# One of three Strassen weight tiles made in DRAM by adding copies instead of on DVE, in a fp32 transformer-layer kernel

## The chip, the cores and the metric

The kernel runs on one core of a Trainium2 chip. The metric is the time of one execution on the device in microseconds, median of three runs. Beside the timed runs there is one profiled execution, from which every row below comes. Engines are named as the profile names them: PE does matmuls (PEld loads their stationary operand), DVE elementwise vector work, ACT activations and copies, POOL a little elementwise work and one DMA queue (q0), SP nothing but the other DMA queue (q1).

## The reference

One layer of a transformer-like trunk on x of 256 x 2048 in fp32: a normalised input projection, two mixers (a gated linear recurrence and chunked attention), gates, an output projection, and a SwiGLU feed-forward block. Cut to the products that matter here:

```
h = rms_norm(x, norm_mix)
proj = h @ w_in                               # 2048 x 11264, the last 4096 columns are gate logits
gate_a, gate_b = split(sigmoid(proj[gates] + b_gate))
merged = gate_a * (y_a @ w_proj_a) + gate_b * (y_b @ w_proj_b)
x = x + merged @ w_out                        # 2048 x 2048
h = rms_norm(x, norm_ffn)
ff_gate, ff_up = split(h @ w_ffn_in)          # 2048 x 11264
x = x + (silu(ff_gate) * ff_up) @ w_ffn_out   # 5632 x 2048
```

## The kernel before, in words

All large products stream their weights from DRAM in tiles of 128 partitions x 2 x 512 floats (512 KB, `raw`, 8 buffers), fetched by SP (`fetch`, L130). A fp32 product is made of three reduced-precision matmuls: each operand is split into a high half `hi` (a copy by ACT, L177) and a low half `lo` (a subtraction by DVE, L178), and `triple` issues hi x hi, hi x lo, lo x hi (L222 to L224). The activation side is the stationary operand, so a matmul streams 512 columns of weights. `hi` and `lo` of the weights have 4 buffers each.

A block of work is a chunk: four k-tiles of a 512-column block of weights. `product` does 24 matmuls for each chunk and each 512 columns. `product_pair` takes two column blocks at once and, on some chunks, replaces the eight triples of k-tiles 0 and 1 by seven, by a scheme of Strassen's kind. This use of the scheme needs sums of four weight blocks. In the names of `weight_forms`: b11 and b21 are k-tiles 0 and 1 of the first column block, b12 and b22 those of the second. Three of the seven weight operands are b11, b21 and b22 themselves, two are in a tile `ta` (b12-b11 and b22-b12) and two in a tile `tb` built from `ta`. DVE makes all four sums (L194, one instruction for each half of a tile), and each tile is then split into `hi` and `lo` like a fetched one. `ta` and `tb` share a pool `t6` of two buffers. On the activation side `act_forms` makes four sums for each use, kept for the whole stretch; the feed-forward ones are stored to DRAM (L315) and loaded again (L907) by POOL's queue.

There are 46 uses: 8 in two gate pairs (4 chunks each), 4 in the first out pair, 20 in the five `w_fi` pairs j = 1, 3, 5, 7, 9 (4 chunks each; the even j are plain products of the same length between them), and 14 in the two `w_fo` pairs (7 of 11 chunks each). In the profiled execution the PE work of these pairs starts at 407 and 492 us (gates), 623 (out), 757, 843, 930, 1017 and 1104 (`w_fi`), 1190 and 1312 (`w_fo`). In all but the `w_fo` pairs the first chunk's plain half is done before its seven triples (`plain_first`).

The order of instructions on each engine is fixed when the program is built: a scheduler places them by priority and by a time model; weight preparation has a raised priority (`PREP_AHEAD`). A buffer is fetched anew when the last reader of its old content is done, and SP issues its DMAs strictly in their order, waiting at each for its buffer.

Of the kernel before, what the change touches and what calls it, by code (L numbers as in the profile page):

```python
# [45 lines left out]
def block_kernel(ctx: ExitStack, tc: tile.TileContext, x, x_t, w_in, w_pa, w_pb, w_out, w_fi, w_fo,  # L46
# [53 lines left out]

    def rsqrt_mean(dst, ss, n):
# [22 lines left out]
    def fetch(w, nb, kc, n=2, pinned=False):  # L124

        res = []
        for hf in range(2):
            raw = wraw_p.tile([P, 2, 512], F32, tag="raw", name=nm("raw"))
# [6 lines left out]
        return res  # L135

# [51 lines left out]
    def weight_forms(r0, r1):  # L188


        ta = t6_p.tile([P, 2, 512], F32, tag="t6", name=nm("ta"))
        tb = t6_p.tile([P, 2, 512], F32, tag="t6", name=nm("tb"))
        b11, b21, b12, b22 = r0[:, 0, :], r0[:, 1, :], r1[:, 0, :], r1[:, 1, :]
        op = lambda out, x, y, o: nc.vector.tensor_tensor(out=out, in0=x, in1=y, op=o)  # L194
        p1, p2 = halves(r0)
        p3, = halves(r1[:, 1:2, :])
# [8 lines left out]
    def product_pair(w, nbs, n_chunks, act, forms, c_pool, u_pool, epilogue, plain_first=False,  # L205
                     last=False):

        tag = {id(mm): "mm", id(aux): "bank"}  # L210
# [36 lines left out]
        for kc in range(n_chunks):  # L247
            end = kc == n_chunks - 1
            early = plain_first and kc == 0
            with tc.high_priority(offset=min(PREP_AHEAD, tc.cur_priority - first_block[0])):  # L250
                r = [fetch(w, nb, kc) for nb in nbs]
                ws = [[None] * 4 for _ in nbs]
                if kc not in forms:
                    for n in range(2):
                        ws[n][0:2] = halves(r[n][0])
                        ws[n][2:4] = halves(r[n][1])
                else:
                    if not early:
                        tf = weight_forms(r[0][0], r[1][0])
                    for n in range(2):  # L260
                        ws[n][2:4] = halves(r[n][1])
                    if early:
                        tf = weight_forms(r[0][0], r[1][0])
# [43 lines left out]
    def transpose_split(nat, hi, lo, gain=None, wait=2, pool=aux, forms=None, spill=None):  # L307
        for _ in range(wait):
            yield 1
        for pair in range(2):  # L310
            pt = transpose_split_pair(nat, pair, hi, lo, gain, pool)
            if forms is not None and pair == 0:
                act_forms(pt, forms, gain)
                if spill is not None:
                    nc.gpsimd.dma_start(out=spill, in_=forms.bitcast(F32))  # L315
            yield 1

    def act_forms(pt, f, gain=None):

# [10 lines left out]
        if gain is None:  # L330
            nc.scalar.copy(s[:, 2, :], a21)
        else:
            nc.scalar.activation(s[:, 2, :], a21, AF.Copy, scale=gain[:, 0:1])
        op(s[:, 0, :], a22, 1, s[:, 2, :], ALU.add)
        op(s[:, 2, :], a11, 0, s[:, 2, :], ALU.subtract)
# [654 lines left out]
```

## Time and profile before

| | |
|---|---|
| median of three runs | 1428.98 us (1428.71 to 1429.38) |
| the profiled execution, time and span | 1427.22 us, 1425.4 us |
| PE / PEld / DVE / ACT / POOL busy | 1417.6 / 1174.4 / 1063.6 / 774.2 / 50.1 us |
| SP's queue q1, POOL's queue q0 | 274.66 MB, 12.58 MB |
| share of the 16 DMA engines, q1 / q0 | 57.5% / 2.3% |

The span is the time from the first to the last instruction of the profiled execution; that execution's own time is 1.8 us more, and lies 1.8 us below the median. Busy time is summed over a whole execution; where an engine that is not the busiest one makes PE wait shows only in windows, waits and timelines.

### The profile page before, as it was taken

How to read it: one execution, taken by the hardware profiler on the slowest of the kernel's cores; microseconds unless marked ns; L12 is line 12 of the kernel's file. 1: busy time of each engine (PE TensorE's matmuls, PEld its weight loads, DVE VectorE, ACT ScalarE, POOL GpSimd, SP SyncE). 2: the span in 40 equal slices, each digit the busy share in tenths (PEclk: the TensorE clock that was granted, in tenths of full speed). 3: DMA queues.
4: the chain of work that ended last, by engine and by line, in shares of the span. 5: the costliest groups of instructions: out<-in, count | busy, mean ns of one | idle time of the engine just before them, and what ended most of it. 6: DMA issues, size and time to landing. Idle time of an engine off the chain costs nothing.

```text
span 1425.4 us, 17596 instructions
## 1 busy us (share of the span) xinstructions
PE 1417.6 (99%) x6448; PEld 1174.4 (82%) x6448; DVE 1063.6 (75%) x1361; ACT 774.2 (54%) x1009; POOL 50.1 (4%) x63
## 2 busy tenths in 40 slices
PE   9999999999999999999999999999999999999998
PEld 7888888888888888878888888888788888888887
DVE  6768869564878697689767769687796876777875
ACT  7756565555655454455555546455454554544553
POOL 0100100100000000100000000000000010000000
PEclk9999999999999999999999999999999999999999
DMA  9654354446657556547654657656476578666652
GB/s 360 243 192 161 134 193 156 164 163 195 222 183 240 197 197 210 184 148 239 220 203 168 228 169 240 206 179 228 164 238 206 178 254 303 210 221 221 208 183 84
DMA packets 81848, 288.37 MB, mean 202 GB/s; under 512 B 9185, under 2 KB 9441, under 8 KB 81761
## 3 DMA queue, kind: packets, MB, share of 16 engines
q1 hardware_dynamic: 78272, 274.66, 57.5%
q0 software_dynamic: 3488, 12.58, 2.3%
q8 instruction: 50, 0.82, 0.2%
q14 instruction: 38, 0.30, 0.1%
HBM read 279.34 MB, written 7.86 MB: 201 GB/s over the span
## 4 chain that ended last, share of the span: by engine, by line
PE 98%; DVE 1%; ACT 0%; DMA 0%; issue 0%; SPq 0%; DVEq 0%; ACTq 0%
PE mm L169 18%; PE mm L168 18%; PE mm L170 18%; PE mp L223 13%; PE mp L224 13%; PE mp L222 13%; PE bank L285 2%; PE bank L543 1%; DVE wlo L178 1%; ACT whi L177 0%; PE bank L573 0%; DMA raw<-in_w_in 0%; PE bank L619 0%; PE bank L670 0%; PE bank L698 0%; DVE tb L194 0%
## 5 line engine op out<-in xcount | busy, mean ns | idle before, releaser
L148 DVE TENSOR_TENSOR wlo<-raw,whi 128x1024 fp32r<-128x1024 f32 (+1 forms) x292 | 351.9, 1212 | 175.6 <-ACT whi L147 173.4
L147 ACT CAST whi<-raw 128x1024 fp32r<-128x1024 f32 (+1 forms) x292 | 301.9, 1040 | 292.7 <-PE mm L170 219.8
L178 DVE TENSOR_TENSOR wlo<-raw,whi 128x1024 fp32r<-128x1024 f32 x216 | 235.0, 1110 | 51.9 <-ACT whi L177 50.8
L177 ACT CAST whi<-raw 128x1024 fp32r<-128x1024 f32 x216 | 201.2, 960 | 121.8 <-PE mp L224 59.6
L168 PE MATMUL mm<-whi,xTh 128*128 128x512 f32 x576 | 226.6, 398 | 1.3 <-ACT whi L147 1.3
L169 PE MATMUL mm<-wlo,xTh 128*128 128x512 f32 x576 | 225.2, 391 | 0.0
L170 PE MATMUL mm<-whi,xTl 128*128 128x512 f32 x576 | 225.1, 391 | 0.0
L168 PE MATMUL mm<-whi,x2Th 128*128 128x512 f32 x384 | 150.0, 391 | 0.0
L170 PE MATMUL mm<-whi,x2Tl 128*128 128x512 f32 x384 | 149.5, 389 | 0.0
L169 PE MATMUL mm<-wlo,x2Th 128*128 128x512 f32 x384 | 149.4, 389 | 0.0
L168 PEld LDWEIGHTS mm<-whi,xTh 128*128 128x128 f32 x576 | 108.2, 188 | 23.0 <-ACT whi L147 2.0
L170 PEld LDWEIGHTS mm<-whi,xTl 128*128 128x128 f32 x576 | 108.2, 188 | 22.6
L169 PEld LDWEIGHTS mm<-wlo,xTh 128*128 128x128 f32 x576 | 108.3, 188 | 21.8 <-DVE wlo L148 1.0
L223 PE MATMUL mp<-wlo,hTh 128*128 128x512 f32 x282 | 109.7, 389 | 0.0
L224 PE MATMUL mp<-whi,hTl 128*128 128x512 f32 x282 | 109.6, 389 | 0.0
L222 PE MATMUL mp<-whi,hTh 128*128 128x512 f32 x282 | 99.7, 390 | 0.0
L177 ACT CAST whi<-ta 128x1024 fp32r<-128x1024 f32 x46 | 48.3, 1050 | 89.9 <-PE mp L224 87.4
L178 DVE TENSOR_TENSOR wlo<-ta,whi 128x1024 fp32r<-128x1024 f32 x46 | 56.2, 1223 | 48.3 <-ACT whi L177 48.3
L224 PE MATMUL mp<-whi,x2Tl 128*128 128x512 f32 x220 | 86.2, 392 | 0.0
L223 PE MATMUL mp<-wlo,x2Th 128*128 128x512 f32 x220 | 86.2, 392 | 0.0
L170 PEld LDWEIGHTS mm<-whi,x2Tl 128*128 128x128 f32 x384 | 72.1, 188 | 15.0
L168 PEld LDWEIGHTS mm<-whi,x2Th 128*128 128x128 f32 x384 | 72.1, 188 | 14.8
(256 smaller groups left out, 2260.8 us busy)
## 6 DMA issues: line engine op xcount, KB each, us to landing
raw<-in_w_fi SPq DMA_DIRECT2D x176, 512.0 KB, 4.4
raw<-in_w_in SPq DMA_DIRECT2D x172, 512.0 KB, 4.1
raw<-in_w_fo SPq DMA_DIRECT2D x88, 512.0 KB, 5.3
raw<-in_w_out SPq DMA_DIRECT2D x32, 512.0 KB, 4.3
raw<-in_w_pa SPq DMA_DIRECT2D x16, 512.0 KB, 3.7
raw<-in_w_pb SPq DMA_DIRECT2D x16, 512.0 KB, 4.3
x<-x POOLq DMA_DIRECT2D x8, 512.0 KB, 5.7
kept<-sform POOLq DMA_DIRECT2D x7, 512.0 KB, 4.9
```

Source lines behind the costliest of these rows:

```text
L147: nc.scalar.copy(hi[:, sl, :], src[:, sl, :])
L148: nc.vector.tensor_tensor(out=lo[:, sl, :], in0=src[:, sl, :], in1=hi[:, sl, :].bitcast(F32), op=ALU.subtract)
L168: nc.tensor.matmul(ps[m], lhsT=ah, rhs=wh, start=kc == 0 and k4 == 0, stop=False)
L169: nc.tensor.matmul(ps[m], lhsT=ah, rhs=wl, start=False, stop=False)
L170: nc.tensor.matmul(ps[m], lhsT=al, rhs=wh, start=False, stop=kc == n_chunks - 1 and k4 == 3)
L177: nc.scalar.copy(hi, src)
L178: nc.vector.tensor_tensor(out=lo, in0=src, in1=hi.bitcast(F32), op=ALU.subtract)
L222: nc.tensor.matmul(ps, lhsT=ah, rhs=wh, start=first, stop=False)
L223: nc.tensor.matmul(ps, lhsT=ah, rhs=wl, start=False, stop=False)
L224: nc.tensor.matmul(ps, lhsT=al, rhs=wh, start=False, stop=final)
L285: nc.tensor.transpose(out=pt[:, j, m * P:(m + 1) * P], in_=nat[:, m, c:c + P], identity=ident)
L543: nc.tensor.matmul(pl[:, j, :], lhsT=ek[:, g // 2, (g % 2) * P:(g % 2 + 1) * P], rhs=eq[:, g, :], start=True, stop=True)
```

## The change

The tile `ta` is no longer made by DVE. `make_sums`, on POOL's queue, makes it in DRAM: for each use two copies of 256 KB from the weights to a DRAM tile (L160), then one DMA of 512 KB that adds the two k-tiles of the second block onto it (L162). To make this possible every sum is a plain addition. It is called at the start of a pair for a later pair, behind a small copy on POOL that waits for a result of the pair that ended (`begin_mark`): at the start of gate pair 1 for out, of gate pair 3 for `w_fi` j = 1, of out for j = 3, of j = 1, 3, 5 for j = 5, 7, 9, and of j = 7 and 9 for the two `w_fo` pairs, 7 uses each; the gates' own sums are made before them. `fetch_pair` then takes five `raw` buffers for a use where there were four: k-tiles 0 and 1 of the first block, b22 alone (256 KB), the finished sum from DRAM, and the two plain halves.

```diff
+    def make_sums(n, mark):
+        pinned = tc.keep_in_program_order
+        if to_make:
+            pinned(nc.gpsimd.tensor_copy(begin_mark, mark))
+        for _ in range(min(n, len(to_make))):
+            name, w, nbs, chunks = to_make.pop(0)
+            for kc in chunks:
+                t = sums_t[name, nbs[0], kc] = dram.tile(
+                    [P, 2, 512], F32, tag=f"sum_{name}{nbs[0]}_{kc}", name=nm("sum"))
+                for n in range(2):
+                    pinned(nc.gpsimd.dma_start(out=t[:, n, :], in_=w[nbs[n], kc, :, 0, :]))
+            for kc in chunks:
+                pinned(nc.gpsimd.dma_start(out=sums_t[name, nbs[0], kc],
+                                           in_=w[nbs[1], kc, :, 0:2, :], accum_op=ALU.add))
+    def fetch_pair(name, w, nbs, kc):
+        b1, b22, ta = raw_tile(), raw_tile(), raw_tile()
+        nc.sync.dma_start(out=b1, in_=w[nbs[0], kc, :, 0:2, :])
+        nc.sync.dma_start(out=b22[:, 1, :], in_=w[nbs[1], kc, :, 1, :])
+        nc.sync.dma_start(out=ta, in_=sums_t[name, nbs[0], kc])
+        rest = []
+        for nb in nbs:
+            rest.append(raw_tile())
+            nc.sync.dma_start(out=rest[-1], in_=w[nb, kc, :, 2:4, :])
+        return (ta, b1, b22), rest
...
-        op(ta[:, 0, :], b12, b11, ALU.subtract)
-        op(ta[:, 1, :], b22, b12, ALU.subtract)
         p5, p7 = halves(ta)
-        op(tb[:, 0, :], ta[:, 0, :], b22, ALU.subtract)
-        op(tb[:, 1, :], b21, tb[:, 0, :], ALU.add)
+        add(tb[:, 0, :], ta[:, 0, :], b22[:, 1, :])
+        add(tb[:, 1, :], b1[:, 1, :], tb[:, 0, :])
...
+        make_sums(1, mark)
...
-                    nc.gpsimd.dma_start(out=spill, in_=forms.bitcast(F32))
+                    nc.sync.dma_start(out=spill, in_=forms.bitcast(F32))
...
-        op(s[:, 0, :], a22, 1, s[:, 2, :], ALU.add)
+        op(s[:, 0, :], a22, 1, s[:, 3, :], ALU.subtract)
...
-        add(e01, ub[6], e00)
-        add(e10, ub[7], e01)
+        sub(e01, ub[6], e00)
+        sub(e10, e01, ub[7])
...
-            nc.gpsimd.dma_start(out=xs[nb], in_=x2_kept[nb])
+            nc.sync.dma_start(out=xs[nb], in_=x2_kept[nb])
```

The other lines of the diff swap additions and subtractions one for one where results are put together, and move the loads of x for the gates' forms, the stores of x2, and the reloads of the stored forms from POOL's queue to SP's, as the two pairs of lines above do.

In the program's order the change shows at pair j = 5 on DVE. Before, between the splits of chunk 0's `ta` and chunk 1's `tb` (`hTl` is the low half of the transposed previous block):

```order
L178 TENSOR_TENSOR wlo_7755<-ta_7742,whi_7754 128x1024 [waits Activation_49]
L194 TENSOR_TENSOR ta_7839<-raw_7835,raw_7831 128x512 [waits DMAHW7_49,DMAHW1_49,DVE_49]
L194 TENSOR_TENSOR ta_7839<-raw_7835 128x512
L295 TENSOR_TENSOR hTl_7724<-bank_7778,hTh_7723 128x512 [waits Activation_49]
L178 TENSOR_TENSOR wlo_7761<-tb_7743,whi_7760 128x1024 [waits Activation_49]
L295 TENSOR_TENSOR hTl_7724<-bank_7799,hTh_7723 128x512 [waits Activation_49]
L194 TENSOR_TENSOR tb_7840<-ta_7839,raw_7835 128x512 [waits DVE_49]
L178 TENSOR_TENSOR wlo_7842<-raw_7831,whi_7841 128x1024 [waits Activation_49]
L178 TENSOR_TENSOR wlo_7846<-raw_7835,whi_7845 128x512 [waits Activation_49]
L194 TENSOR_TENSOR tb_7840<-raw_7831,tb_7840 128x512 [waits DVE_49]
L178 TENSOR_TENSOR wlo_7852<-ta_7839,whi_7851 128x1024 [waits Activation_49]
L178 TENSOR_TENSOR wlo_7858<-tb_7840,whi_7857 128x1024 [waits Activation_49]
```

and after, from the split of chunk 0's sum (raw_7845) to that of chunk 1's `tb` (tb_7957); raw_8029, raw_8030 and raw_8031 are b1, b22 and the sum of chunk 2:

```order
L218 TENSOR_TENSOR wlo_7871<-raw_7845,whi_7870 128x1024 [waits Activation_49]
L332 TENSOR_TENSOR hTl_7824<-bank_7894,hTh_7823 128x512 [waits Activation_49]
L218 TENSOR_TENSOR wlo_7877<-tb_7861,whi_7876 128x1024 [waits Activation_49]
L332 TENSOR_TENSOR hTl_7824<-bank_7915,hTh_7823 128x512 [waits Activation_49]
L99 TENSOR_TENSOR tb_8039<-raw_8031,raw_8030 128x512 [waits DMAHW6_49,DMAHW5_49,DVE_49]
L218 TENSOR_TENSOR wlo_7959<-raw_7947,whi_7958 128x1024 [waits Activation_49]
L218 TENSOR_TENSOR wlo_7963<-raw_7948,whi_7962 128x512 [waits Activation_49]
L99 TENSOR_TENSOR tb_8039<-raw_8029,tb_8039 128x512 [waits DMAHW4_49,DVE_49]
L218 TENSOR_TENSOR wlo_7967<-raw_7949,whi_7966 128x1024 [waits Activation_49]
L218 TENSOR_TENSOR wlo_7973<-tb_7957,whi_7972 128x1024 [waits Activation_49]
```

The two `ta` subtractions of chunk 1 are gone, and the place of chunk 1's first `tb` operation is taken by chunk 2's, which now waits for DMAs; chunk 1's four splits stand behind it as before.

PE's order there is the same in both but for the numbers; these are the matmuls that take the low halves of chunk 1's `ta` (wlo_7852) and `tb` (wlo_7858), as before has them:

```order
L223 MATMUL mp_7816<-wlo_7852,fx_5593 128x512 [waits DVE_49]
L224 MATMUL mp_7816<-whi_7851,fx_5593 128x512
L223 MATMUL mp_7820<-wlo_7852,fx_5593 128x512
L224 MATMUL mp_7820<-whi_7851,fx_5593 128x512
L222 MATMUL mp_7764<-whi_7861,x2Th_5591 128x512 [waits Activation_49]
L223 MATMUL mp_7824<-wlo_7858,fx_5593 128x512 [waits DVE_49]
```

Nothing moves there; the DVE instructions that they wait for now stand behind the waiting addition.

On POOL's queue a `w_fi` pair now begins with this, after, at the start of j = 1 (sums 6398 to 6407 are those of the four chunks of j = 5); before, POOL had one store of forms (L315) in such a pair or none:

```order
L153 COPY begin_mark<-hn_6243 128x1 [waits DVE_49]
L160 DMA sum_6398<-in_w_fi 128x512 x2
L160 DMA sum_6401<-in_w_fi 128x512 x2
L160 DMA sum_6404<-in_w_fi 128x512 [waits DMASW0_49]
L160 DMA sum_6404<-in_w_fi 128x512 [waits DMASW1_49]
L160 DMA sum_6407<-in_w_fi 128x512 [waits DMASW2_49]
L160 DMA sum_6407<-in_w_fi 128x512 [waits DMASW3_49]
L162 DMA sum_6398<-in_w_fi 128x1024 [waits DMASW5_49,DMASW4_49]
L162 DMA sum_6401<-in_w_fi 128x1024 [waits DMASW7_49,DMASW6_49]
L162 DMA sum_6404<-in_w_fi 128x1024 [waits DMASW1_49,DMASW0_49]
L162 DMA sum_6407<-in_w_fi 128x1024 [waits DMASW3_49,DMASW2_49]
```

Each adding DMA waits on POOL until its own two copies have landed. The sum of chunk 2 is fetched by SP (raw_8031) into the buffer of raw_7845, which is free once the first instruction of the DVE piece of after above, the split into wlo_7871, has read it.

## Rows read from the trace of the kernel before

**Rows 1.** The page of the whole execution: span, engines' busy time, granted clock, DMA queues.

```profile
span 1425.4 us, 17596 instructions
...
PE 1417.6 (99%) x6448; PEld 1174.4 (82%) x6448; DVE 1063.6 (75%) x1361; ACT 774.2 (54%) x1009; POOL 50.1 (4%) x63
...
PEclk9999999999999999999999999999999999999999
...
q1 hardware_dynamic: 78272, 274.66, 57.5%
```

**Rows 2.** Windows: us, busy us (instructions) of PE, PEld, DVE, ACT, POOL; clock, DMA share.

```profile
0.00:454.00 454.00, 451.54 (x2128) 378.31 (x2129) 328.50 (x493) 274.50 (x436) 23.92 (x32) 1.00 0.58 199
628.00:669.00 41.00, 40.78 (x180) 32.07 (x179) 38.70 (x50) 24.98 (x31) 0.00 (x0) 1.00 0.54 179
846.00:888.00 42.00, 41.46 (x186) 33.48 (x185) 38.09 (x48) 25.85 (x30) 0.53 (x1) 1.00 0.60 196
1019.00:1061.00 42.00, 41.45 (x186) 33.54 (x185) 37.47 (x47) 25.55 (x30) 0.53 (x1) 1.00 0.58 197
1148.00:1199.00 51.00, 51.00 (x233) 42.31 (x232) 31.86 (x37) 22.61 (x26) 5.93 (x11) 1.00 0.86 315
1312.00:1425.00 113.00, 109.42 (x483) 90.31 (x481) 81.25 (x90) 52.07 (x54) 0.00 (x0) 1.00 0.50 167
```

**Rows 3.** Weight loader's waits, 836 to 860: us in total, times, longest.

```profile
PEld mp L222 <- ACT whi L177: 1.2, 2, 1.0
```

**Rows 4.** The same view, 628 to 645.

```profile
PEld mp L223 <- DVE wlo L178: 1.1, 2, 0.5
```

**Rows 5.** DVE by line and form: count | busy us, mean ns | idle before, released by.

```profile
L178 DVE TENSOR_TENSOR wlo<-raw,whi 128x1024 fp32r<-128x1024 f32 x170 | 204.2, 1221 | 45.3 <-ACT whi L177 44.2 <-DMA raw<-in_w_fi 0.2
...
L194 DVE TENSOR_TENSOR ta<-raw,raw 128x512 f32<-128x512 f32 x46 | 32.1, 697 | 15.8 <-DMA raw<-in_w_fi 8.2 <-DMA raw<-in_w_fo 4.3 <-DMA raw<-in_w_in 1.8
L194 DVE TENSOR_TENSOR ta<-raw 128x512 f32<-128x512 f32 x46 | 31.5, 685 | 0.0
```

**Rows 6.** DVE timeline in pair j=5: start us, duration us, instruction [idle before <- releaser].

```profile
930.24 1.41 DVE L862 SCALAR_TENSOR_TENSOR hn<-mm,r,hn 128x512 f32<-128x512 f32 x2
...
934.53 1.23 DVE L178 TENSOR_TENSOR wlo<-ta,whi 128x1024 fp32r<-128x1024 f32 x1 [2.29 <-ACT whi L177]
...
939.70 0.68 DVE L194 TENSOR_TENSOR tb<-ta,raw 128x512 f32<-128x512 f32 x1
940.30 1.82 DVE L178 TENSOR_TENSOR wlo<-raw,whi 128x1024 fp32r<-128x1024 f32 x2
942.04 0.69 DVE L194 TENSOR_TENSOR tb<-raw,tb 128x512 f32<-128x512 f32 x1
942.64 1.22 DVE L178 TENSOR_TENSOR wlo<-ta,whi 128x1024 fp32r<-128x1024 f32 x1
943.92 1.23 DVE L178 TENSOR_TENSOR wlo<-tb,whi 128x1024 fp32r<-128x1024 f32 x1
```

**Rows 7.** PE timeline there, same columns: two matmuls with a lo half.

```profile
944.62 0.39 PE L223 MATMUL mp<-wlo,fx 128*128 128x512 f32 x1
...
945.75 0.39 PE L223 MATMUL mp<-wlo,fx 128*128 128x512 f32 x1
```

**Rows 8.** SP's weight fetches of pair j=5 (930 to 1020): issue ns, landing us.

```profile
L130 SPq DMA_DIRECT2D raw<-in_w_fi x34: 327/328/328, 930.3 to 1018.5; - x34
...
DMA to landing us min/median/max: 3.5/4.5/6.1
```

**Rows 9.** The same line from 1160 to 1192, beside POOL's reloads.

```profile
DMA to landing us min/median/max: 4.5/8.3/8.9
```

**Rows 10.** DMA view 1160 to 1192: packets, MB, share of the 16 engines.

```profile
q1 hardware_dynamic: 1549, 5.65, 47.3%
q0 software_dynamic: 1436, 5.24, 43.2%
```

**Rows 11.** POOL timeline, 1160 to 1204: three issues in a row.

```profile
1164.70 1.74 POOL L907 DMA_DIRECT2D sf<-kept  x3
```

More of the change, by code (lines that the diff above doesn't have):

```diff
@@ L99, in add, with sub @@
         nc.vector.tensor_tensor(out=out, in0=a, in1=b, op=ALU.add)
+    def sub(out, a, b):
+        nc.vector.tensor_tensor(out=out, in0=a, in1=b, op=ALU.subtract)
     def rsqrt_mean(dst, ss, n):
@@ L250, in product_pair @@
             with tc.high_priority(offset=min(PREP_AHEAD, tc.cur_priority - first_block[0])):
-                r = [fetch(w, nb, kc) for nb in nbs]
                 ws = [[None] * 4 for _ in nbs]
                 if kc not in forms:
+                    r = [fetch(w, nb, kc) for nb in nbs]
                     for n in range(2):
@@ L328, in op @@
                                                op0=ALU.mult, op1=o)
[L330 to L333, printed above, removed]
-        op(s[:, 0, :], a22, 1, s[:, 2, :], ALU.add)
-        op(s[:, 2, :], a11, 0, s[:, 2, :], ALU.subtract)
-        op(s[:, 1, :], a11, 0, s[:, 0, :], ALU.subtract)
-        op(s[:, 3, :], a12, 1, s[:, 1, :], ALU.add)
+        nc.scalar.activation(s[:, 3, :], a21, AF.Copy, scale=1.0 if gain is None else gain[:, 0:1])
+        op(s[:, 0, :], a22, 1, s[:, 3, :], ALU.subtract)
+        op(s[:, 2, :], a11, 0, s[:, 3, :], ALU.subtract)
+        op(s[:, 1, :], a11, 0, s[:, 0, :], ALU.add)
+        op(s[:, 3, :], a12, 1, s[:, 1, :], ALU.subtract)
         split(f[:, 0], f[:, 1], s)
@@ L737, in block_kernel @@
         start(hgrn_mix(half, b, kk, qT, v, sg, *yaT[half]))
+    to_make += [("in", w_in, (14 + nb, 18 + nb), range(4)) for nb in SEVEN_GATE]
+    to_make += [("out", w_out, (2 * i, 2 * i + 1), range(4)) for i in SEVEN_OUT]
+    to_make += [("fi", w_fi, (j, NJ + j), range(4)) for j in SEVEN_IN]
+    to_make += [("fo", w_fo, (2 * i, 2 * i + 1), SEVEN) for i in range(2)]
     for half in range(2):
@@ L758, in x_forms @@
             xt = t4([P, 2, T], "xt2")
-            nc.gpsimd.dma_start(out=xt, in_=x_t[c, :, 0:2, :])
+            nc.sync.dma_start(out=xt, in_=x_t[c, :, 0:2, :])
             fq[c] = t4([P, 2, 4, P], "fq", F32R)
@@ L785, in sums @@
                 four_sums(ub, *(gates[br, nb][:, m, :] for br in range(2) for m in range(2)))
-            cb = product_pair(w_in, (14 + nb, 18 + nb), 4, act_x, fq, aux, mm, sums,
-                              plain_first=True, last=True)
+            cb = product_pair("in", w_in, (14 + nb, 18 + nb), 4, act_x, fq, aux, mm, sums,
+                              gates[1, nb - 1][:, 0, 0:1], plain_first=True, last=True)
             for br in range(2):
@@ L847, in block_kernel @@
         if pair in SEVEN_OUT:
-            cb = product_pair(w_out, nbs, 4, act_m, fm, aux, mm,
-                              residual_sums(xs[nbs[0]], xs[nbs[1]]), plain_first=True, last=True)
+            cb = product_pair("out", w_out, nbs, 4, act_m, fm, aux, mm,
+                              residual_sums(xs[nbs[0]], xs[nbs[1]]), gates[1, 3][:, 0, 0:1],
+                              plain_first=True, last=True)
             for n, nb in enumerate(nbs):
@@ L871, in sums @@
             four_sums(ub, hn[:, 0, :], hn[:, 1, :], *u)
-        cb = product_pair(w_fi, (j, NJ + j), 4, act_x2, fx, aux, mm, sums, plain_first=True,
-                          last=True)
+        cb = product_pair("fi", w_fi, (j, NJ + j), 4, act_x2, fx, aux, mm, sums, hn_before[:, 0, 0:1],
+                          plain_first=True, last=True)
         for m in range(2):
-            add(hn[:, m, :], cb[m, 0], hn[:, m, :])
+            (sub if m == 1 else add)(hn[:, m, :], cb[m, 0], hn[:, m, :])
             nc.scalar.activation(hn[:, m, :], hn[:, m, :], AF.Silu, scale=r2[:, m:m + 1])
@@ L906, in block_kernel @@
         forms[j] = t4([P, 2, 4, P], "sf", F32R)
-        nc.gpsimd.dma_start(out=forms[j].bitcast(F32), in_=kept[j])
+        nc.sync.dma_start(out=forms[j].bitcast(F32), in_=kept[j])
     for pair in range(2):
@@ L911, in block_kernel @@
         for nb in nbs:
-            nc.gpsimd.dma_start(out=xs[nb], in_=x2_kept[nb])
+            nc.sync.dma_start(out=xs[nb], in_=x2_kept[nb])
         x0, x1 = (xs[nb] for nb in nbs)
         pools = (mm, aux) if pair == 0 else (aux, mm)
-        cb = product_pair(w_fo, nbs, NJ, act_h, forms, *pools,
-                          residual_sums(x0, x1), last=pair == 1)
+        cb = product_pair("fo", w_fo, nbs, NJ, act_h, forms, *pools,
+                          residual_sums(x0, x1), hn[:, 0, 0:1], last=pair == 1)
         for n, nb in enumerate(nbs):
```

48 lines of the change are left out of this document (26 added, 22 removed).

## The prediction

> **What bounds the kernel now.** I read the page first, then a table of windows, then the waits of PE and DVE, then single stretches on timelines. The page says that PE is busy for 1417.6 of 1425.4 us, at a full granted clock in all 40 slices [rows 1]. So the most that any change off PE can give back is 7.8 us. The windows say where those 7.8 us lie: 2.46 in the first 454 us and 3.58 in the last 113 [rows 2], at the start and the end of the program, which this change does not reach. What is left in the pairs is idle PE of 0.22, 0.54 and 0.55 us in the out pair and in j = 3 and j = 7 [rows 2]. The waits show it a little larger, since a matmul whose operand is late is partly shown as a long matmul: PE's weight loader waited 1.2 us for weight halves at the start of j = 3 [rows 3], j = 7 shows the same figure, and 1.1 us at the start of out [rows 4]. Together between 1.3 us (idle) and 3.5 us (waits). These are the places where DVE is busiest (38 to 39 of 41 to 42 us [rows 2]): the forms of the activations are made there. So DVE bounds nothing but three short stretches, and a gain is at most 3.5 us.
>
> **The change, part by part.**
>
> *What DVE loses.* 46 x (697 + 685) ns = 63.6 us of `ta` subtractions [rows 5]; DVE falls from 1063.6 to about 1000 us. PE runs beside all of it, so this is worth nothing outside the three stretches. Worth there: 0 to -3.5 us.
>
> *Signs.* Additions and subtractions change places one for one, on the same engines: 0.
>
> *Fetches on SP.* A use takes five DMAs for four, and 26 loads and stores move over from POOL: some 72 issues more at 328 ns [rows 8] = 24 us on a queue that has 1425 and spends them waiting for buffers. By issue time 0. But eight buffers now hold 1.6 uses instead of two, so a fetch starts later against its use. That is the term that matters, and it is worked out next.
>
> *The wait of chunk 2's addition.* In the order of before, chunk 1's first `tb` operation needs only what DVE itself made just ahead of it. In the order of after, that place is taken by chunk 2's (`tb_8039`), and what it needs is a sum that SP fetches into the buffer that the split of chunk 0's sum (`wlo_7871`) frees, four DVE instructions ahead. All that stands behind it on DVE waits with it: the four splits that give the low halves of chunk 1's seven triples. I take pair j = 5, where PE lost nothing before, and lay the new order on the old timeline. The split of chunk 0's `ta` runs from 934.53 to 935.76 [rows 6]; with 0.1 us for SP to see it (my allowance) the fetch goes out at 935.86 and lands L later. DVE would be free for the addition at about 939.7, since the place in the row is the same. From the addition to the end of the split of `tb` before took 939.70 to 945.15 = 5.45 us, the same six instructions as after [rows 6]. So with a late landing that split ends at 935.86 + L + 5.45 = 941.31 + L. PE takes the low half of `ta` at 944.62 and that of `tb` at 945.75 [rows 7]. The second is met if L is under 4.44 us; for the first, the split ends 1.29 us earlier (943.86 against 945.15), at 940.02 + L, which is met under 4.6. Beyond that PE stands for **L - 4.4 us**, once in the pair.
>
> The other seven pairs that begin with a plain half (two gates, out, the other four of `w_fi`) have the same piece of order, in some with one or two DVE instructions more or fewer between release and addition. In j = 3, j = 7 and out DVE is fuller, so the wait hurts from a smaller L; but what PE lost there before is lost in the same place and not twice. Counted out alike these come to L - 4.3 to L - 4.5 net, so I take 8 x (L - 4.4) for all, an estimate. The `w_fo` pairs have seven triples ahead of the plain half and no such crowding: 0, with 3 us as an upper bound for two pairs.
>
> *How long L is.* In a quiet stretch a fetch lands after 3.5 to 6.1 us, 4.5 in the median [rows 8]. Where POOL's reloads ran beside it, the median was 8.3 and the worst 8.9 [rows 9]; there q1 took 47.3% and q0 43.2% of the engines and together they moved 10.89 MB in 32 us, which is 376 GB/s at full use [rows 10]. Which of these holds when chunk 2's sum is fetched? POOL's burst begins when the last `hn` of the pair before is done, at 930.24 + 1.41 = 931.65 [rows 6]. POOL issues a DMA in 1.74 / 3 = 0.58 us [rows 11], so its eight copies go out until 936.3. They carry 2.1 MB, 5.6 us of all engines at that rate, and the four adding DMAs follow with 2.1 MB more, counted once. The fetch at 935.86 lies in the middle of it. By this it should be near 8.3; but the burst is younger and shorter than the reloads there, and the low end of the loaded stretch was 4.5. I take the slowest landing of the quiet stretch, **L = 6.1**, which is near the middle of the two medians, and keep 4.5 and 8.3 as ends.
>
> The Trainium skill has a rule that speaks against this change: by "DMA: Bandwidth & Descriptors", section "Issuing engines are not separate DMA queues", transfers issued by SP and by GpSimd run on the same 16 engines and interleave. The trace agrees, with landings of 8.3 us beside POOL's traffic against 4.5 without it; with queues that don't disturb each other the sum would be +0.8 us, with the loaded landing +31.
>
> *The sum.* 8 x (6.1 - 4.4) = +13.6 us, in which the three old stalls are counted; 4.5 gives +0.8, 8.3 gives +31.2. On the profiled execution's 1427.2 that is 1440.8; the median of the runs shown lies 1.8 higher, so **1442.6**.
>
> *POOL.* The burst's own waits (each adding DMA for its two copies) hold up what is behind it on POOL: the small powers for the norm and the gates' additions. A burst of 4.2 MB at half of 376 GB/s is over after 22 us, one of 7.3 MB after 39, and nothing there is wanted before the pair ends, some 43 us after it starts: 0. The sums are made a whole pair ahead, over 80 us for `w_fi`, so none is late: 0, unless bandwidth fails (below).
>
> *Loads moved to SP.* A reload that waits on SP for PE holds all fetches behind it. Before, they waited on POOL, where nothing was behind them that SP needed. The fetches around 1190 would start some us later, with eight full buffers ahead: 0 to 2 us; I take 0.
>
> **The rivals.**
>
> *B: the bursts starve the weights for as long as they last.* A burst of four uses is 2.1 MB of copies and 2.1 of adding DMAs, twice that for the latter if the target has to be read as well: 4.2 to 6.3 MB. For seven uses (in j = 7 and j = 9) it is 7.3 to 11.0. A pair's own weights are 4 chunks x 4.5 x 0.524 = 9.4 MB in 43.5 us = 217 GB/s. If q0 and q1 share 376 GB/s evenly while a burst lasts, the weights get 188, 13% too little, for 6.3 / 0.188 = 33 us or 58 us: 4.5 us in each of six pairs and 7.7 in two, +42, on top of the forecast: some +56, 1485. For it: the loaded stretch ran at 376 GB/s with landings doubled. Against it: PE lost nothing there (51.00 of 51.00 at a DMA share of 0.86 [rows 2]), and the weights' eight buffers are full when a burst begins. It decides if an adding DMA takes far more engine time for each byte than a reload. No row of before has one.
>
> The Trainium skill says in "Collectives: The Full Stack", section "Why ReduceScatter is half of AllGather", that an add in the DMA engines needs two source reads and so moves at half the rate of a copy. No row of this kernel before shows it; by it the larger of the two byte counts would be the right one.
>
> *C: hidden.* L stays under about 4.7 where it counts, since the engines serve two queues in turn and the fetch is only 0.5 MB. Then the sum is within 2.9 us of nothing (0.2%, about what a measurement of this kernel can tell from no change): -2 to +2.9, around 1429. For it: the median landing of 4.5 in quiet stretches, and at 1148 to 1199 no loss despite landings of 8.3. Against it: there was lead there, and here there is none to spare.
>
> *D: faster.* The freed DVE time ends the stalls in out, j = 3 and j = 7, and the sum lands in 4.0 us or less everywhere, inside what the quiet stretch shows (3.5 at best): -1.3 to -3.5, at best 1425.5. It decides below L = 4.3. Only its upper part would be measured as faster.
>
> **How the numbers follow.** The forecast (L between 4.8 and 8.9, 1432 to 1465) gets 0.52, B 0.18, C 0.20, D 0.10. The range of 1427 to 1472 leaves out D, a small part of C, and most of B. Faster 0.10, same 0.20, slower 0.70.
>
> **What the profile after would show.** If the forecast is right: DVE busy near 1000 us and yet a new wait on DVE, the first `tb` addition (L99) for a DMA, eight long events of about 2 us (941.96 against 939.7), one some 9 us after the start of each pair; PE idle or stretched by 1 to 3 us some 15 us after each start, waiting for `wlo` (L218); landings of the sums' fetches of 5 to 8 us there, and 4 to 5 in plain blocks. If B is right, landings stay over 8 us long after the burst's start, SP's fetches are late throughout j = 7 and j = 9, and q0's share is well over 15%. If C or D is right, the loads of the sums land in under 4.7 us in spite of the burst, or the addition is late and PE does not notice. The prediction fails if the scheduled order is not what decides: if PE has more lead at that place than the one pair that I laid out shows, or if adding DMAs are far dearer than reloads.

## The result, and the profile after

The changed kernel took 1506.25 us in the median of four runs (1503.88 to 1508.84), against 1429.18 us for the kernel before beside it: a ratio of 1.0538 with a 95% interval of 1.0518 to 1.0558, 5.4% slower. The forecast was 1442.6, with a range of 1427 to 1472.

The page of the changed kernel, with the parts that answer to [rows 1], the chain of work and waits that ended last, the line of the waiting addition, and the DMA issues (size, median landing):

```profile
span 1502.1 us, 17890 instructions
...
PE 1441.1 (96%) x6448; PEld 1190.6 (79%) x6448; DVE 1011.4 (67%) x1269; ACT 774.6 (52%) x1009; POOL 124.8 (8%) x185
...
q1 hardware_dynamic: 88640, 299.31, 58.2%
q0 software_dynamic: 13984, 48.24, 14.1%
...
PE mm L209 16%; PE mm L210 16%; PE mm L208 16%; PE mp L259 10%; PE mp L260 10%; PE mp L258 9%; DMA raw<-sum 8%; DVE wlo L218 2%; DMA bias<-in_bias 2%; PE bank L322 1%; ACT whi L217 1%; PE bank L578 1%; DMA raw<-in_w_fi 1%; DMA raw<-in_w_out
...
L99 DVE TENSOR_TENSOR tb<-raw,raw 128x512 f32<-128x512 f32 x46 | 32.5, 707 | 95.3 <-DMA raw<-sum 89.2
...
raw<-in_w_fi SPq DMA_DIRECT2D x156, 512.0 KB, 4.9
...
raw<-sum SPq DMA_DIRECT2D x46, 512.0 KB, 4.2
...
sum<-in_w_fi POOLq DMA_DIRECT2D x40, 256.0 KB, 8.6
sum<-in_w_fi POOLq DMA_DIRECT2D x20, 512.0 KB, 10.4
```

The account of the 76.7 us of span is in the first two lines. PE was idle for 7.8 us before and for 61.0 now, 53.2 more; and its busy time rose from 1417.6 to 1441.1, 23.5 more, for the same 6448 instructions. So two thirds are waiting and one third is PE running slower. DVE fell to 1011.4 as meant. Its first `tb` addition, which waited for no DMA before, now waits 95.3 us, 89.2 of them for the fetch of a sum, and the chain that ended last has 8% of the span in that fetch. The same line before:

```profile
L194 DVE TENSOR_TENSOR tb<-ta,raw 128x512 f32<-128x512 f32 x46 | 31.5, 684 | 0.0
```

PE's waits (us in total, times, longest) say what the idle time is:

```profile
PE mp L259 <- DVE wlo L218: 43.9, 12, 6.1
PE bank L741 <- ACT pT L734: 7.2, 2, 4.2
PE mp L258 <- ACT whi L217: 2.9, 1, 2.9
```

Where it was lost, from the start of each stage's matmuls on PE's timeline in both traces (us lost since the stage before):

| stage | lost in it |
|---|---|
| up to the first gate pair: start of the program, attention | 1.5 and 9.3 |
| gate pairs 1 and 3 | 6.3 and 7.0 |
| out pair | 5.1 |
| `w_fi` pairs j = 1, 3, 5 | 6.8, 6.5, 7.3 |
| `w_fi` pairs j = 7, 9 (bursts of seven sums) | 14.6 and 11.6 |
| plain blocks between them, and `w_fo` | under 0.5 each |

The 1.5 us are lost before 20 us, while the first weights land. Every version below loses 0.3 to 2.7 us there against the profiled execution before (which lies 1.8 us under its median), also those that make no sums, so I don't count them to the change.

Pair j = 5, on DVE's timeline, answers to [rows 6]; in this trace it starts at 973.0, 42.5 us later than before:

```profile
977.00 1.23 DVE L218 TENSOR_TENSOR wlo<-raw,whi 128x1024 fp32r<-128x1024 f32 x1 [2.30 <-ACT whi L217]
...
980.42 1.23 DVE L218 TENSOR_TENSOR wlo<-tb,whi 128x1024 fp32r<-128x1024 f32 x1 [0.26 <-ACT whi L217]
981.57 0.68 DVE L332 TENSOR_TENSOR hTl<-bank,hTh 128x512 fp32r<-128x512 f32 x1
988.47 0.69 DVE L99 TENSOR_TENSOR tb<-raw,raw 128x512 f32<-128x512 f32 x1 [6.22 <-DMA raw<-sum]
989.08 1.82 DVE L218 TENSOR_TENSOR wlo<-raw,whi 128x1024 fp32r<-128x1024 f32 x2
990.82 0.68 DVE L99 TENSOR_TENSOR tb<-raw,tb 128x512 f32<-128x512 f32 x1
991.42 1.22 DVE L218 TENSOR_TENSOR wlo<-raw,whi 128x1024 fp32r<-128x1024 f32 x1
```

The split of chunk 0's sum ends at 978.23, SP issues chunk 2's sum at 978.3, 5.3 us after the pair's start, and the addition stands ready at 982.2 and waits 6.22 us. On PE the first low half that is missed is that of chunk 1's b11 and b21:

```profile
990.35 0.80 PE L259 MATMUL mp<-wlo,x2Th 128*128 128x512 f32 x1 [4.93 <-DVE wlo L218]
...
991.37 0.63 PE L259 MATMUL mp<-wlo,x2Th 128*128 128x512 f32 x1
...
994.79 0.50 PE L259 MATMUL mp<-wlo,fx 128*128 128x512 f32 x1
995.12 0.39 PE L260 MATMUL mp<-whi,fx 128*128 128x512 f32 x1
```

PE stood 4.93 us, and after it a matmul took 0.63 us and began 0.43 us after the one ahead, until 994.79; from then 0.39 and 0.23. The windows (columns as in [rows 2]) show the granted clock at that time:

```profile
984.00:988.00 4.00, 1.42 (x7) 0.84 (x5) 0.00 (x0) 1.07 (x2) 1.08 (x2) 1.00 1.00 278
988.00:992.00 4.00, 1.65 (x4) 1.36 (x5) 3.53 (x5) 0.00 (x0) 1.35 (x2) 0.52 1.01 169
992.00:996.00 4.00, 4.00 (x13) 3.16 (x12) 4.00 (x4) 2.44 (x3) 0.05 (x1) 0.62 1.04 268
996.00:1000.00 4.00, 4.00 (x19) 3.29 (x19) 1.87 (x3) 1.57 (x3) 0.00 (x0) 1.00 1.04 275
```

It was 1.00 until PE stood still and 0.52, the lower of the two levels (1.2 of 2.4 GHz), where PE took up work again, and it was back at 1.00 within 5 us of work. The DMA share in the same windows is 1.00 to 1.04: the 16 engines are full.

### The profile page after: what moved, and what is told of

Same layout as the page of the kernel before. It is cut to its first block, busy times and chain, and to the rows that moved or that the text cites. A ratio compares the mean times of both kernels' runs of the same rounds, so it can differ in the third digit from the quotient of the medians.

```text
span 1502.1 us, 17890 instructions
## 1 busy us (share of the span) xinstructions
PE 1441.1 (96%) x6448; PEld 1190.6 (79%) x6448; DVE 1011.4 (67%) x1269; ACT 774.6 (52%) x1009; POOL 124.8 (8%) x185
## 3 DMA queue, kind: packets, MB, share of 16 engines
q0 software_dynamic: 13984, 48.24, 14.1%
## 4 chain that ended last, share of the span: by engine, by line
PE 81%; DMA 12%; DVE 3%; ACT 2%; issue 2%; SPq 0%; DVEq 0%; POOL 0%; ACTq 0%; POOLq 0%
PE mm L209 16%; PE mm L210 16%; PE mm L208 16%; PE mp L259 10%; PE mp L260 10%; PE mp L258 9%; DMA raw<-sum 8%; DVE wlo L218 2%; DMA bias<-in_bias 2%; PE bank L322 1%; ACT whi L217 1%; PE bank L578 1%; DMA raw<-in_w_fi 1%; DMA raw<-in_w_out 0%; PE bank L608 0%
## 5 line engine op out<-in xcount | busy, mean ns | idle before, releaser
L188 DVE TENSOR_TENSOR wlo<-raw,whi 128x1024 fp32r<-128x1024 f32 (+1 forms) x292 | 351.5, 1211 | 181.8 <-ACT whi L187 180.9
L187 ACT CAST whi<-raw 128x1024 fp32r<-128x1024 f32 (+1 forms) x292 | 302.0, 1039 | 284.0 <-PE mm L210 214.9
L217 ACT CAST whi<-raw 128x1024 fp32r<-128x1024 f32 (+1 forms) x262 | 250.7, 977 | 254.3 <-PE mp L260 151.6
L218 DVE TENSOR_TENSOR wlo<-raw,whi 128x1024 fp32r<-128x1024 f32 (+1 forms) x262 | 289.4, 1129 | 99.6 <-ACT whi L217 98.6
L259 PE MATMUL mp<-wlo,x2Th 128*128 128x512 f32 x220 | 90.0, 409 | 28.8 <-DVE wlo L218 28.8
L99 DVE TENSOR_TENSOR tb<-raw,raw 128x512 f32<-128x512 f32 x46 | 32.5, 707 | 95.3 <-DMA raw<-sum 89.2
L260 PE MATMUL mp<-whi,x2Tl 128*128 128x512 f32 x220 | 89.3, 406 | 0.0
L217 ACT CAST whi<-tb 128x1024 fp32r<-128x1024 f32 x46 | 48.3, 1049 | 76.1 <-PE mp L260 71.5
```

The source lines that it names most:

```text
L99: nc.vector.tensor_tensor(out=out, in0=a, in1=b, op=ALU.add)
L187: nc.scalar.copy(hi[:, sl, :], src[:, sl, :])
L188: nc.vector.tensor_tensor(out=lo[:, sl, :], in0=src[:, sl, :], in1=hi[:, sl, :].bitcast(F32), op=ALU.subtract)
L217: nc.scalar.copy(hi, src)
L218: nc.vector.tensor_tensor(out=lo, in0=src, in1=hi.bitcast(F32), op=ALU.subtract)
L259: nc.tensor.matmul(ps, lhsT=ah, rhs=wl, start=False, stop=False)
```

## The experiments

Theory A: the traffic of the sums delays SP's fetch of chunk 2's sum, whose lead is too short, and the order alone costs next to nothing. The lead is the time from a fetch's issue until its reader on DVE stands ready; here that is 4.0 to 4.4 us. Its rivals: the order costs by itself (B); it is the adding that loads the DMA engines (C); the engines are short of time wherever the bursts lie (D). All kernels are the changed one but for the edit, of which the main lines are shown, and are compared with runs of the kernel before beside them. What a stage lost is read from the start of its matmuls on PE's timeline, as above.

**1. No sums made.** The third tile comes straight from the weights, and POOL's copy into `begin_mark` goes too.

```diff
-        nc.sync.dma_start(out=ta, in_=sums_t[name, nbs[0], kc])
+        nc.sync.dma_start(out=ta, in_=w[nbs[1], kc, :, 0:2, :])
...
-        for _ in range(min(n, len(to_make))):
+        for _ in range(0):
```

> POOL makes no sums; the third tile of each use is fetched straight from the weights (wrong numbers, same bytes on SP, same place of the waiting addition on DVE). Theory A (the sums' traffic delays SP's fetches; the order alone costs almost nothing): landings back to 4 to 5 us, the long waits before the chunk-2 addition gone, granted clock 1.00, 1426 to 1433 us. Theory B (five buffers for each use and the addition put ahead of chunk 1's splits cost by themselves): PE still stands 2 us or more in each of eight pairs, 1445 us or more.

Measured: 1433.99 us, ratio 1.0042 (1.0029 to 1.0055). The traffic is worth 72 of the 77 us. But theory A asked for 1433 at most with almost no cost of the order, and 5.0 us were lost in the eight pairs: nothing in the first gate pair, 0.2 to 1.5 us in each of the others. Its waits on PE:

```profile
PE mp L259 <- DVE wlo L218: 4.6, 8, 1.5
```

They are not where theory A looks. Chunk 2's tile landed in 3.6 to 4.0 us, and its addition waited for nothing in seven of the eight pairs (1.1 us in out). The next one, chunk 3's, waited 1.6 to 4.8 us in every pair, and in six of them PE stood behind it for 0.2 to 1.5 us, 24 to 26 us after the start. On DVE in j = 5, which starts at 934.8 in this trace:

```profile
944.14 0.69 DVE L99 TENSOR_TENSOR tb<-raw,raw 128x512 f32<-128x512 f32 x1
...
957.27 0.69 DVE L99 TENSOR_TENSOR tb<-raw,raw 128x512 f32<-128x512 f32 x1 [3.82 <-DMA raw<-in_w_fi]
```

**2 and 3. Copies without adds; copies in place of adds.** Run 2 leaves the 46 adding DMAs out. Run 3 keeps DVE's order and POOL's, and drops only the adding:

```diff
-                                           in_=w[nbs[1], kc, :, 0:2, :], accum_op=ALU.add))
+                                           in_=w[nbs[1], kc, :, 0:2, :]))
```

> The 46 adding DMAs are left out, the 92 copies of 256 KB stay (wrong numbers). Theory A: half the traffic; the copies still run when chunk 2's sum is fetched, so a stall of 1 to 4 us stays in each of the eight pairs, and the loss in the attention, j = 7 and j = 9 shrinks to a third: 1445 to 1470 us. Theory C (it is the adding that loads the DMA engines): close to no traffic at all, under 1436 us.

> Each adding DMA of 512 KB becomes a plain copy of 512 KB to the same place (the numbers are wrong, and DVE's order is the same as in the changed kernel). Theory A, bytes between two places in DRAM count whether added or not: 1490 to 1506 us, chunk-2 landings of 9 to 10 us as before it. Theory C, an add costs twice a copy: the stall at chunk 2 is the same (only copies are ahead of it), but j = 7, j = 9 and the attention recover half of their 37 us: 1480 to 1490 us.

Measured: 1478.85 us, ratio 1.0352 (1.0336 to 1.0368), and 1484.15 us, ratio 1.0399 (1.0380 to 1.0417). Run 2 came out above both expectations: with the copies alone 50 of the 77 us stay, 45 more than in run 1, since they are what runs when chunk 2's sum is fetched. The eight pairs lost 2.9 to 8.4 us each in it, the attention nothing beyond 2.5 at the start of the program. Run 3 fell into the range of theory C. The page's queue lines price the adding; q0 in run 2 and in run 3:

```profile
q0 software_dynamic: 7360, 24.12, 5.4%
```

```profile
q0 software_dynamic: 13984, 48.24, 10.2%
```

5.4% of 1476.8 us is 79.7 us of all 16 engines for 24.1 MB of copies of 256 KB, and the further 24.1 MB of copies of 512 KB took 10.2% of 1482.3 less that, 71.5 us. In the changed kernel the adds of the same bytes took 14.1% of 1502.1 less 79.7, 132.1 us: 1.85 times a copy, if the copies of 256 KB take the same in all three. The attention, without the start of the program, lost 1.1 us with copies for adds, 9.3 with adds.

**4. The bursts in the plain blocks.**

```diff
-        make_sums(1, mark)
...
+            make_sums(1, r2[:, 0:1] if j == 0 else hn[:, 0, 0:1])
             ps = product(w_fi, j, 4, act_x2)
```

The second part stands where an even j begins, and likewise in the gates, the projections and out.

> Same sums, same traffic, but each burst starts with the plain block between two pairs (second half of the gates' and out's blocks, even j), not with a pair. Theory A with the short lead as the place where it hurts: the 5 us stalls of seven pairs vanish, plain blocks ride most of it out on their eight buffers, the attention's 11 us stay: 1440 to 1465 us. Theory D (engine time is short wherever the burst is): the stalls only move into the plain blocks, 1490 us or more.

Measured: 1469.24 us, ratio 1.0282 (1.0268 to 1.0296), between the two and in neither range. The stalls in the pairs went down to 3.3 us or less. But a burst lasts 32 to 38 us for four uses and 51 to 53 for seven, and what a plain block saved was lost where the burst ran into the fetches of the next pair's first chunks (9.9 us of waiting on DVE ahead of j = 1).

**5. The sums on DVE again,** by two additions, with the signs, the moved loads and stores, and `fetch_pair`'s order of fetches kept.

```diff
+        add(ta[:, 0, :], b22[:, 0, :], b1[:, 0, :])
+        add(ta[:, 1, :], b22[:, 1, :], b22[:, 0, :])
         p5, p7 = halves(ta)
```

> No sum is made in DRAM; DVE makes the third tile again, by two additions into its old pool, four buffers for a use; the swapped signs and the loads and stores moved to SP stay. Theory A, all of the loss and the 5.5 us of the run without sum traffic come from the five buffers, the fetched sum and its traffic: 1427 to 1430 us. Rival: the moved loads and stores or the signs cost part of those 5.5 us: 1431 to 1435 us.

Measured: 1433.76 us, ratio 1.0034 (1.0021 to 1.0047), so the rival, by the number. By stages it lost 2.0 us at the start of the program, nothing in the attention, 0.2 in all pairs up to 1190 us and 4.1 in `w_fo`. The pairs' 5.0 us of run 1 thus do belong to the five buffers; the 4.1 come neither from the signs nor from the moved loads and stores but from the order of the fetches (run 9).

**6. The burst 15 us later in the same pair.**

```diff
-        make_sums(1, mark)
...
+            if kc == 2:
+                make_sums(1, ws[0][3][1][:, 0:1].bitcast(F32))
```

> Same bursts in the same pairs, begun when chunk 2's weights are prepared, some 15 us later. Theory A (what costs most is that the copies run while chunk 2's sum is fetched): the 5 us stalls at chunk 2 in the six small pairs vanish; j = 7, j = 9 and the attention keep theirs, since the burst is as long: 1445 to 1470 us. Theory D (engine time is short wherever the burst lies): 1490 us or more, with new stalls in chunk 3 and in the plain blocks.

Measured: 1453.14 us, ratio 1.0157 (1.0140 to 1.0174), as theory A had it. In the profiled execution, the longest of the four at 1459.97 us, the eight pairs lost 2.3 us at most, j = 7 and j = 9 too, which I had expected to keep their loss. The plain blocks after them lost up to 4.2 (j = 6, beside a burst of seven), `w_fo` 3.8, and the attention 11.4. Chunk 2's sum landed in 3.1 to 4.4 us.

**7. One sum at a time,** at 48 marks: two copies for one use, the add for the use before.

```diff
+        if half_made:
+            name, w, nbs, kc = half_made.pop()
+            pinned(nc.gpsimd.dma_start(out=sums_t[name, nbs[0], kc],
+                                       in_=w[nbs[1], kc, :, 0:2, :], accum_op=ALU.add))
+        if todo:
...
+            for n in range(2):
+                pinned(nc.gpsimd.dma_start(out=t[:, n, :], in_=w[nbs[n], kc, :, 0, :]))
```

> Same sums and bytes, but never a burst: at 48 marks, one in each plain product and two in the second half of each pair, two copies for one use and the add for the use before. Theory A (the backlog that a burst builds up is what delays SP's fetches): landings stay under 7 us, no stall over 1.5 us, granted clock near 1.00, 1434 to 1442 us, that is the 5.5 us of the order and little more. Theory D (it is the total of engine time): 1460 us or more.

Measured: 1450.56 us, ratio 1.0151 (1.0137 to 1.0166), worse than theory A and better than D. The `w_fi` and gate pairs lost 0.9 us at most; 8.3 us went in the attention and 9.6 in the out pair. I took this for POOL's queue, because ahead of out POOL stood 4 to 11 us at almost every adding DMA, waiting for its copies, with the gates' additions (L859) behind. But PE waited for those only this long:

```profile
PE bank L332 <- POOL gate L859: 0.8, 1, 0.8
```

What stopped it in out is a sum's fetch again. POOL issued an adding DMA and two copies at 637.6 to 638.7 us, SP fetched chunk 2's sum at 644.5, and it landed after 6.8 us. DVE and PE there:

```profile
651.43 0.69 DVE L99 TENSOR_TENSOR tb<-raw,raw 128x512 f32<-128x512 f32 x1 [5.82 <-DMA raw<-sum]
...
653.32 0.80 PE L267 MATMUL mp<-wlo,mTh 128*128 128x512 f32 x1 [6.22 <-DVE wlo L227]
```

In the attention two of the four bias tiles landed after 9.3 and 10.3 us (4.5 to 5.7 before).

**8 and 9. Only six sums from DRAM,** chunks 0 and 1 of out, j = 3 and j = 7, one at a time; run 9 with the fetches of the other 40 uses as in the kernel before (the last two lines).

```diff
+    MADE = lambda name, nb, kc: (name, nb) in (("out", 0), ("fi", 3), ("fi", 7)) and kc < 2
...
+        if not MADE(name, nbs[0], kc):
+            r = [fetch(w, nb, kc) for nb in nbs]
+            return (None, r[0][0], r[1][0]), [r[0][1], r[1][1]]
```

> As the one-by-one version, but only six uses take their sum from DRAM: chunks 0 and 1 of out, j = 3 and j = 7, where DVE was too busy before; the other 40 are made by DVE. If the three old stalls come from DVE's load alone and a sum that is ready in time ends them: 1424.5 to 1427.5 us, the only gain there is. If the fetched sum is late even without a burst, because its buffer comes free late: 1428 to 1431 us.

> The six-sums version, but the 40 uses that DVE makes are fetched in the order of the kernel before (each block's two tiles together). In the six-sums run the pairs up to 1190 us stood within 1 us of before and the last stage lost 5 us. If the order of fetches did that: 1427 to 1429.5 us, with the out pair 0.6 us shorter and j = 3 and j = 7 unchanged. If the loads moved to SP did it: 1432 to 1435 us again.

Measured: 1433.35 us, ratio 1.0032 (1.0020 to 1.0045), and 1433.08 us, ratio 1.0033 (1.0021 to 1.0045). No gain, and neither range of run 8's expectation: the out pair was 0.6 us shorter in run 8, and that is all. In j = 3 and j = 7 PE lost what it lost before; its waits in j = 3 of run 9 answer to [rows 3]:

```profile
PEld mp L275 <- ACT whi L230: 1.4, 1, 1.4
```

The `w_fo` stage lost 5.1 us in run 8 and nothing in run 9, so the order of the fetches did that. (Run 9 also allots the tile `ta` ahead of `tb`, but so does run 5, which lost 4.1 there.) Run 9 lost 0.7 us at the start of the program, 2.2 in the attention and 1.5 in out, so my expectation for the whole was wrong. What costs the 2.2 and the 1.5 stays open: run 8 makes the same sums at the same places and lost neither.

**10. Same bursts, more lead for chunk 2.** Chunks 0 and 1 of the eight pairs don't use their sums (`MADE` is `name == "fo" or kc >= 2`; the sums are made all the same).

> All sums are made in DRAM as in the changed kernel, burst for burst, but chunks 0 and 1 of the eight pairs don't use theirs (DVE makes them, four buffers a use). Chunk 2's sum then goes into a buffer that comes free 11 to 13 us of DVE work ahead of its addition, not 2.4. Theory A (short lead against a landing of 10 us): the 5 us stalls at chunk 2 vanish though the traffic is the same; the attention's 11 us and much of j = 7 and j = 9 stay: 1445 to 1465 us. Theory D (engine time is short, whatever the lead): 1485 us or more.

Measured: 1488.51 us, ratio 1.0422 (1.0408 to 1.0435), by the numbers theory D. The timeline of DVE in j = 1 says what happened:

```profile
791.34 0.68 DVE L99 TENSOR_TENSOR tb<-raw,raw 128x512 f32<-128x512 f32 x1
...
808.23 0.69 DVE L99 TENSOR_TENSOR tb<-raw,raw 128x512 f32<-128x512 f32 x1 [9.61 <-DMA raw<-sum]
```

Chunk 2's addition (791.34) no longer waits. But this is no test of a longer lead against the same landing: chunk 2's fetch now goes out 0.2 us ahead of the pair's start, before the first copy of the burst, and lands in 3.1 to 3.6 us in all pairs. Chunk 3's addition now stands ready 4.3 us after its fetch went out, where it had 9.5 us in the changed kernel, and waits 9.61 us for a sum that was fetched amid the adds and took 13.9 us to land. So the wait ended where the fetch was out of the burst's way; the short lead had moved on, into the dearer half of the burst.

**11. Only the `w_fi` sums, one at a time, from the out pair on;** the rest on DVE with the fetches of before (`MADE` is `name == "fi"`).

> Only the 20 sums of the five w_fi pairs come from DRAM, made one by one from the out pair on, when the attention and the gates are done; the other 26 are made by DVE, with the fetches of before. In the one-by-one run w_fi pairs lost under 1 us each, and 19 of its 22 us were lost in the attention and in out, where POOL itself had work behind waiting DMAs. If that is POOL's queue: 1428.5 to 1432 us here. If the traffic itself costs: 1434 us or more.

Measured: 1439.58 us, ratio 1.0068 (1.0047 to 1.0089), runs from 1431.5 to 1442.6, so the traffic, in the median. Nothing was lost up to j = 1 but 0.5 us at the start of the program; then 4.7 us in j = 1 and 6.5 in j = 3, and nothing in j = 5 and j = 9. There one use's copies and add (1 MB) happened to be under way at the place of chunk 2's fetch, which then landed after 8.0 and 9.2 us (3.1 to 3.4 in the three other pairs). What run 7 lost in out was thus this and not POOL's queue; the first of j = 3's waits on DVE:

```profile
862.59 0.69 DVE L99 TENSOR_TENSOR tb<-raw,raw 128x512 f32<-128x512 f32 x1 [4.91 <-DMA raw<-sum]
```

**12. Half the copies.**

```diff
-                for n in range(2):
+                for n in range(1):
...
-        nc.sync.dma_start(out=ta, in_=sums_t[name, nbs[0], kc])
+        nc.sync.dma_start(out=ta[:, 0, :], in_=sums_t[name, nbs[0], kc][:, 0, :])
+        nc.sync.dma_start(out=ta[:, 1, :], in_=w[nbs[1], kc, :, 1, :])
```

> One copy of 256 KB for each sum tile instead of two, no adds; the other half of the tile is fetched from the weights as a DMA of its own (wrong numbers). In the run with both copies chunk 2's fetch, issued 5.3 us after the pair's start as ever, landed 7.0 to 10.8 us later; without any it landed after 3.6 to 4.0. Backlog theory: four copies are issued by 3.5 us and mostly done when the fetch goes out, so it lands after 5 to 6.5 us and a pair stalls for 1 to 2 us: 1438 to 1450 us. Rival (any copy within DRAM beside it slows a fetch to the same degree): landings of 8 us or more, 1465 us or more.

Measured: 1450.40 us, ratio 1.0157 (1.0140 to 1.0174), 0.4 us above the range of the backlog theory. Issued at 5.2 or 5.3 us after the start in all of these, chunk 2's fetch landed after:

| copies issued by POOL by then | landing in the eight pairs, us |
|---|---|
| none (run 1) | 3.6 to 4.0 |
| 4, and no more (run 12, six pairs) | 5.0 to 6.5 |
| 4, and 4 more within some 4 us (out and first gate pair of run 2, out of the changed kernel) | 7.0, 9.8 and 7.2 |
| 7 (run 12, j = 7 and j = 9) | 8.8 and 7.0 |
| 7 (run 2, six pairs) | 8.0 to 10.8 |
| 6 or 7 (changed kernel, seven pairs) | 7.6 to 10.2 |

The landing grows with what is issued ahead of the fetch, and also with what follows just behind it.

## Why the prediction was wrong, point by point

**The bound, and the gain at most (right, and too generous).** PE bounds the kernel; runs 8 and 9 gave 0.6 of the 3.5 us back, in out of run 8 alone. My reading that DVE's load made the stalls of j = 3 and j = 7 was wrong: with the `ta` work of chunks 0 and 1 gone from there PE's loader still waited 1.4 us, for ACT's half of the split. The row had said so, `<- ACT whi` [rows 3].

**The saving on DVE (sized a little too high).** 63.6 us forecast, 52.2 measured: I took the mean duration of an instruction, but one starts before the last has ended, about 0.6 us after it [rows 6], and it is that spacing which is saved.

**The place of the new wait (right).** The fetch of chunk 2's sum was forecast 5.3 us after the pair's start and went out at 5.3; DVE stands at that addition, and PE at the low halves of chunk 1, in all eight pairs. Runs 6 and 10 take the wait away by putting the burst behind the fetch, or the fetch ahead of the burst.

**L, the step that failed.** I took 6.1 us, from the quiet stretch, with 8.9 as the worst case. The fetch landed after 7.2 to 10.2, 9.3 in the mean. I had worked out that eight copies of 2.1 MB would be on their way to the engines, 5.6 us of their time, when the fetch goes out, and said that the value should be near 8.3; then I took a lower one because the burst is younger and shorter than the reloads of [rows 9]. The copies are also dearer than reckoned: at the rate of run 2, 24.1 MB in 79.7 us, the eight take 6.9 us. Run 12 and the table above show that the landing follows what POOL issues around the fetch. With 9.3 the same formula gives 8 x 4.9 = +39, and the stalls at chunk 2 themselves came near that: the first of each pair, 2.6 to 6.3 us from the start of one matmul to the next beyond the usual 0.23, sum to 36.

L alone doesn't explain the result: +39 would have given 1468, inside the range. What carries the time to 1506 are three terms that the sum had at nothing, told below: the lower clock after the stalls (some 18 us), further stalls in j = 7 and j = 9 (some 12), and the attention (9.3).

**What PE does after a stall (left out).** The forecast priced a stall at its length. All stalls in the pairs but one were followed by some 3 to 6 us of matmuls at the lower level of the clock, at 0.43 us a matmul for 0.23; behind the shortest, the first of j = 9, the clock stayed at 1.00. PE's busy time is 23.5 us longer, some of it in the attention and at the start of the program.

**One stall in a pair (too few).** In j = 7 and j = 9 the burst has seven uses. While the adds ran, 70% of the engines' time went to POOL's queue; the DMA view of 1084 to 1100 in j = 7:

```profile
q0 software_dynamic: 592, 2.15, 70.2%
q1 hardware_dynamic: 467, 1.73, 33.3%
...
raw<-in_w_fi SPq DMA_DIRECT2D x6, 512.0 KB, 20.5
```

With landings of 20 us the weights of chunk 3 came late too, and these pairs lost 14.6 and 11.6 us. (The bursts lasted 46 and 49 us there from the first issue to the last landing, and 27 to 31 in the other six pairs, where the prediction had 39 and 22.) That is rival B's mechanism. It held in these two pairs, for which B had 7.7 us on top of the first stall: beyond that stall (5.4 and 2.6) and the slow matmuls that followed it (some 2 us in j = 7, none in j = 9) it was 7 and 9. In the six others next to nothing was lost after chunk 2, so B as a whole did not hold. The Trainium skill's rule in "Collectives: The Full Stack", section "Why ReduceScatter is half of AllGather", that an add moves at about half the rate of a copy, is borne out: 1.85 times the engine time (runs 2 and 3 against the changed kernel).

**The attention (not seen).** I put POOL's bursts and the moved loads at 0, and looked at them in the pairs only. The sums for the gates are made while the attention runs, whose bias tiles SP fetches between the weights. The landings of these four fetches in the changed kernel, which were 4.5 to 5.7 us before:

```profile
DMA to landing us min/median/max: 4.8/9.8/17.7
```

The two late ones, at 14.6 and 17.7 us, hold up POOL's fill of the same tile, DVE's addition of the bias and at last PE (`PE bank L741 <- ACT pT`): 9.3 us. With copies for adds it was 1.1 us. There is a second cause that I had put at 0: POOL itself stood at the adding DMAs ahead of these fills until 306.9 and 386.3 us, 0.6 and 2.2 us before the tiles landed. In run 7, where no adding DMA waits ahead of the fills, tiles landed after 9.3 and 10.3 us and 8.3 us were lost all the same. How much each adds here is not separated.

**Where lead is there, nothing was lost (right).** `w_fo` lost 0.3 us with sums and moved reloads together.

**The short lead without traffic (right at chunk 2, but a second place left out).** The formula allows 4.4 us, and at 3.6 to 4.0 chunk 2's addition held up PE in no pair of run 1 but out. Most of the 5.0 us of run 1 was lost behind chunk 3's addition. I had laid out one addition of a pair, and not the next, whose fetch goes into the same ring of eight buffers.

The account of the 76.7 us, by stages and the stalls in them: 1.5 at the start of the program, 9.3 in the attention, some 36 in the eight stalls at chunk 2, some 12 in three further stalls of j = 7 and j = 9, and the rest, some 18, at the lower clock after them, less what these pairs had lost before.

No version here beats the kernel before. Runs 8 and 9 point to the reason: the freed DVE time bought 0.6 us at most.

## What to carry to other kernels

Before a job is moved from an engine with time to spare to the DMA engines, ask what the fetches will wait behind, and price a fetch that goes out during a burst at the time that the burst's bytes around it take, those issued ahead of it above all, not at a mean landing. A ring of buffers that is full has little lead: here, with one more buffer a use, the refill went out 4.0 us before its reader stood ready (978.3 and 982.2 in j = 5), and its landing after 10.1 us reached the engine that bounds the kernel. The stall of 5 us on PE then cost 7, by the clock. And ask it for every reader in the stretch, not for the first one.

## What the runs showed of the hardware that was not expected

A DMA that adds within DRAM took 1.85 times the engine time of a copy of the same size there (132.1 against 71.5 us for 24.1 MB). Copies within DRAM moved 24.1 MB in 79.7 us of all engines in pieces of 256 KB, 303 GB/s, and in 71.5 us in pieces of 512 KB, 337 GB/s, against 274.66 MB in 57.5% of 1425.4 us, 335 GB/s, for fetches into the buffers on chip [rows 1]. The two queues did not share the engines' time evenly while sums were added: in 1084 to 1100 us of j = 7, with fetches of SP under way all the time, q0 took 70% and q1 33%. By packets they were closer, 592 and 467: a packet of q0 took 0.30 us of an engine and one of q1 0.18, worked out from these numbers. And a fetch of SP's landed about when the copies issued around it did: in j = 5 the last of the seven copies issued ahead of it at 987.4 us, the fetch at 988.4, and the eighth copy, issued 1.0 us behind the fetch, at 988.4.
